# A depthwise convolution rewritten over odd and even tokens, and one norm moved among attention heads

## The chip, the cores and the metric

The kernel runs on one core of one Trainium2 chip. The metric is device time in microseconds (us) of one execution. Five engines run their own instruction streams and meet at semaphores: TensorE (PE, with its weight loads as PEld), VectorE (DVE), ScalarE (ACT), GpSimd (POOL) and SyncE (SP), whose queue here issues nearly all transfers.

## What is computed

One encoder layer on two sequences, a prompt of 512 tokens and a sample of 256, all in float32. After an RMSNorm, one input projection feeds two groups in parallel: latent attention with 8 heads, and a convolution group of 512 channels. Both are normalised, joined and projected back; a SwiGLU feed-forward block and a last norm follow. The part that is changed is the convolution group:

```python
u = conv_a * jax.nn.sigmoid(conv_g)
u = lax.conv_general_dilated(u, dw_w[:, None, :], window_strides=(1,),
                             padding=[(CONV_PAD, CONV_PAD)],
                             dimension_numbers=("NWC", "WIO", "NWC"),
                             feature_group_count=CONV_CH) + dw_b
u = jax.nn.silu(layer_norm(u, conv_ln_g, conv_ln_b))
merged = jnp.concatenate([rms_norm(attn, attn_out_g), rms_norm(u, conv_out_g)], axis=-1)
return merged @ w_out
```

`dw_w` has 31 taps per channel, and each channel is convolved with its own taps, along the tokens, with 15 zeros at both ends of each sequence.

## The kernel before

Products run on TensorE with each operand split into a high and a low part (`split`, lines 104 to 111: ScalarE rounds the high part, VectorE subtracts to get the low one), three matmuls for each product. Tokens are cut into blocks b of 128 (0 to 3 the prompt, 4 and 5 the sample), channels into four tiles i of 128. The program is written in this order:

- A: the convolution's input projection, channel tile by channel tile. `glu(i)` gates a tile: VectorE writes the gated values to `u[s][i]` (s is 0 for the prompt, 1 for the sample), with zeros around them.
- B: the attention's input projections (`tm_mm`), by block. C: queries, keys and values (`q_up`, `k_up`, `v_up`), and the rotary step `rope` (lines 375 to 378) on VectorE after each `q_up`. When C is done, its pools are closed and the memory is given to tiles of the attention, `qh` and `ql` among them, so that the first `qh` waits for the last `rope`.
- D: the attention in 12 units (`units`): units 0 to 3 are the sample's heads in pairs, units 4 to 11 the prompt's heads. A unit is scores (`pss`, line 293), a row maximum on VectorE (`ngmx`, line 711), the exponential on ScalarE (line 714), transposes (`ptp`, line 731) and the product with the values (`po`). The scores have three PSUM banks. The loop writes `st_q(i + 1)`, `st_s(i)`, `st_t(i - 1)` and, for every second head, `st_v(i - 1)` at step i.
- Between these steps of D stand pieces of the convolution's norm: `conv_ln(b)` (four transposes `pcl` of the convolution's result, statistics `bst` and `mv` on VectorE, a reciprocal root on GpSimd, the normalised `z` on ScalarE), `conv_act1` and `conv_act2` (transposes `pca` back, swish, the sum of squares `prc`), `conv_split`. The prompt's start at step `LN0` = 4. The sample's stand at the end: after the last head come the output products `oc(b, o)` of the prompt's convolution half, with `attn_norm` for the prompt, and the sample's `conv_ln(4)`, `conv_ln(5)`, `conv_act1(1, k)`, `conv_act2(1, k)` and `conv_split(1)` lie among `oc(1, 1)` to `oc(3, 1)`.
- Then `out_conv` and `out_attn` for the remaining blocks into eight `bank` tiles, the second norm, and the feed-forward block, which fills the rest of the run from about 355 us.

The convolution is not matmul work. Each output tile `acc[s][i]` starts as tap 0 times u plus the bias on ScalarE (line 248), and 30 VectorE instructions add one tap each:

```python
for j in range(1, KW):
    yield n / 512, lambda j=j: DVE.scalar_tensor_tensor(a, us[:, j : j + n], w(j), a, ALU.mult, ALU.add)
```

These taps fill VectorE between other work. A generator (`conv_taps`) yields a cost and an instruction; every matmul written through `mm` adds its length times a rate (`RATE`, one for each stage) to an account, and `tap_some` writes taps until the account is used up, in turn from the first `TAPW` generators. `tap_all(s)` writes all that are left. The framework then orders each engine's instructions, by readiness and by the order of writing; only transposes written under `pin` keep their place.

## Time and profile before

| | |
|---|---|
| median of three runs | 846.03 us (843.57 to 849.58) |
| the profiled execution | 845.79 us, span 844.0 us |
| TensorE busy | 810.1 us, 96% of the span |
| VectorE busy | 714.8 us, 85% |
| ScalarE busy | 434.4 us, 51% |
| mean granted TensorE clock | 0.990 |

The span runs from the first to the last instruction; the execution's own time is 1.8 us longer. In a timeline row stand the start, the length, the engine, the line, the operation, output<-input, sizes and the number of instructions merged; in brackets is the idle time before it and what ended it. Rows of stretches give for each engine busy time and instructions, then the granted clock (1.00 is full speed), the share of the DMA engines and GB/s. "Landing" is the time from a transfer's issue to its arrival.

### The profile page before, as it was taken

The page shows a single profiled execution, that of the slowest core. Times are in us where ns is not written, and L with a number is a line of the kernel's source. Part 1 is how long each engine was busy: PE and PEld are TensorE (multiplying, and loading weights), DVE is VectorE, ACT ScalarE, POOL GpSimd, SP SyncE. Part 2 cuts the span into 40 slices and gives each one's busy share as a digit, 9 for nine tenths or more (in the row PEclk, how much of TensorE's full clock was granted, in tenths as well). Part 3 has the DMA queues.
Part 4 walks back from the last instruction along what each step waited for, and adds up shares of the span by engine and source line. Part 5 has one row for each costly group of instructions (what it writes and reads, how often), then busy time and mean ns, then how long its engine had stood idle before and what let it go on. Part 6 is the DMA issues. An engine that isn't in the chain of part 4 may idle for free.

```text
span 844.0 us, 12490 instructions
## 1 busy us (share of the span) xinstructions
PE 810.1 (96%) x4381; PEld 722.9 (86%) x4381; DVE 714.8 (85%) x1310; ACT 434.4 (51%) x886; POOL 87.9 (10%) x113
## 2 busy tenths in 40 slices
PE   6999999879999899999999999999999999999996
PEld 5888998866766678799999999999999988888775
DVE  4699989989898855898999988898988669989993
ACT  6623337958895254784333343433334346455753
POOL 1000341001010201100000000000000000004743
PEclk9999999989999989999999999999999999999999
DMA  8812102300001231368554333444344699963344
GB/s 304 293 54 76 45 1 76 151 1 1 1 1 51 75 101 75 114 203 287 191 196 151 122 127 130 147 144 147 126 151 139 218 306 321 312 205 123 103 138 149
DMA packets 49662, 117.18 MB, mean 139 GB/s; under 512 B 5056, under 2 KB 18368, under 8 KB 49600
## 3 DMA queue, kind: packets, MB, share of 16 engines
q1 hardware_dynamic: 49424, 116.00, 40.9%
q8 instruction: 34, 0.56, 0.3%
q10 hardware_dynamic: 144, 0.39, 0.1%
q14 instruction: 28, 0.23, 0.1%
q0 software_dynamic: 32, 0.00, 0.0%
HBM read 93.96 MB, written 22.41 MB: 138 GB/s over the span
## 4 chain that ended last, share of the span: by engine, by line
PE 54%; DVE 4%; issue 3%; DMA 1%; POOL 1%; ACT 1%; POOLq 0%; ACTq 0%; DVEq 0%
PE bank L293 53%; DVE wr L108 1%; DMA sr<-wdn 1%; DVE sr L1308 1%; DVE ra L108 1%; DVE xall L1214 0%; DVE sa L108 0%; DVE xall L1227 0%; PE bank L982 0%; POOL nmv L969 0%; POOL fmv L1241 0%; POOL fmr L1242 0%; DVE vt L1218 0%; POOL nmr L971 0%; ACT vt L1226 0%
## 5 line engine op out<-in xcount | busy, mean ns | idle before, releaser
L293 PE MATMUL bank<-ra,wr 128*128 128x384 f32 x1056 | 186.6, 335 | 0.0
L293 PEld LDWEIGHTS bank<-ra,wr 128*128 128x128 f32 x1056 | 183.4, 188 | 0.0
L293 PE MATMUL bank<-sa,wr 128*128 128x384 f32 x780 | 139.2, 335 | 0.0
L293 PE MATMUL bank<-wr,wr 128*128 128x512 f32 x594 | 135.1, 389 | 1.3 <-DVE wr L108 1.3
L293 PEld LDWEIGHTS bank<-sa,wr 128*128 128x128 f32 x780 | 135.5, 188 | 0.0
L250 DVE SCALAR_TENSOR_TENSOR acc<-u,c,acc 128x512 f32<-128x512 f32 (+1 forms) x240 | 132.9, 610 | 0.1
L293 PEld LDWEIGHTS bank<-wr,wr 128*128 128x128 f32 x594 | 111.4, 188 | 24.8 <-DVE wr L108 1.7
L107 ACT CAST wr<-vt 128x512 fp32r<-128x512 f32 x88 | 54.6, 620 | 97.7 <-PE bank L293 92.6
L107 ACT CAST wr<-sr 128x512 fp32r<-128x512 f32 x106 | 64.7, 616 | 61.3 <-PE bank L293 60.0
L108 DVE TENSOR_TENSOR wr<-sr,wr 128x512 fp32r<-128x512 f32 x106 | 71.9, 683 | 14.7 <-ACT wr L107 14.7
L1236 POOL TENSOR_SCALAR fme<-fms 128x1 f32<-128x1 f32 x6 | 33.9, 5644 | 418.3 <-ACT vt L1226 418.0
L293 PE MATMUL pc<-ra,sa 128*128 128x256 f32 (+1 forms) x288 | 54.4, 350 | 8.2 <-ACT ra L110 8.2
L108 DVE TENSOR_TENSOR wr<-vt,wr 128x512 fp32r<-128x512 f32 x88 | 60.1, 685 | 0.0
L293 PEld LDWEIGHTS pc<-ra,sa 128*128 128x128 f32 x288 | 45.8, 195 | 15.8 <-ACT ra L110 8.6
L107 ACT CAST wr<-ra 128x384 fp32r<-128x384 f32 x51 | 26.0, 512 | 33.1 <-PE bank L293 21.2
L293 PE MATMUL pss<-ra,qh 96*128 96x512 f32 (+1 forms) x96 | 30.4, 397 | 6.2 <-ACT qh L107 5.3
L108 DVE TENSOR_TENSOR wr<-ra,wr 128x384 fp32r<-128x384 f32 x51 | 28.1, 551 | 8.5 <-ACT wr L107 8.3
L293 PE MATMUL bank<-wr,ra 128*128 128x512 f32 x144 | 34.2, 394 | 0.0
L293 PE MATMUL pq<-sa,ra 128*128 128x384 f32 x108 | 33.8, 342 | 0.0
L711 DVE TENSOR_REDUCE ngmx<-pss 128x1 f32<-128x512 f32 (+1 forms) x40 | 27.0, 685 | 6.2 <-PE pss L293 6.0
L293 PEld LDWEIGHTS bank<-wr,ra 128*128 128x128 f32 x144 | 26.7, 188 | 5.6
L293 PE MATMUL bank<-sa,ra 128*128 128x512 f32 x114 | 30.3, 419 | 0.1
(224 smaller groups left out, 1340.5 us busy)
## 6 DMA issues: line engine op xcount, KB each, us to landing
sr<-wgu SPq DMA_DIRECT2D x52, 512.0 KB, 3.9
sr<-wdn SPq DMA_DIRECT2D x34, 512.0 KB, 4.6
sumd<-xall SPq DMA_DIRECT2D x44, 192.0 KB, 1.9
ra<-sumd SPq DMA_DIRECT2D x44, 192.0 KB, 5.0
actd<-xall SPq DMA_DIRECT2D x11, 384.0 KB, 2.3
xall<-actd SPq DMA_DIRECT2D x11, 384.0 KB, 2.9
st<-wconv SPq DMA_DIRECT2D x7, 512.0 KB, 6.1
xr<-xtok SPq DMA_DIRECT2D x6, 512.0 KB, 6.7
```

Of the source, the lines that this page charges most:

```text
L107: ACT.copy(dst_hi, src)
L108: DVE.tensor_sub(dst_lo, src, dst_hi.bitcast(F32))
L250: yield n / 512, lambda j=j: DVE.scalar_tensor_tensor(a, us[:, j : j + n], w(j), a, ALU.mult, ALU.add)
L293: pinned(PE.matmul(out, lhsT, rhs, start=start, stop=stop))
L711: DVE.tensor_reduce(mx, ps.rearrange("p (j n) -> p j n", j=m), AX.X, ALU.max, negate=True)
L1236: POOL.tensor_scalar(fme[b], fms[:, 2 * b + 1 : 2 * b + 2], 1.0, EPS, ALU.mult, ALU.add)
L1308: DVE.tensor_add(w, tw[f], w)
```

## The change

Let e and o be a channel's even and odd taps (16 and 15), and x0, x1 the gated values at every second position of the padded sequence. The 31-tap convolution is then put together from three of half the length: P = x0 with the even taps, Q = x1 with the odd ones, and S = x0 + x1 with the sums of neighbouring taps. The even outputs are P + Q, the odd ones S - P - Q, each plus the bias. Both sequences lie side by side in one row of 416 positions with 16 zeros between them, so that one instruction over 400 or 401 columns serves prompt and sample.

- `glu(i)` writes each gated piece in two instructions, reading every second column, instead of in one. Line 255 and 256 (`cab`) add neighbouring taps once; they are written at `build_rb` and read only the constants `c`.
- Per channel tile, instead of 30 taps of 512 and 30 of 256 columns: one sum x0 + x1 (416), 15 + 14 + 15 taps of 400, one subtraction (400), and four instructions that write outputs to every second column (two of 256, two of 128). ScalarE starts P, Q and S (three of 400) instead of two accumulators (512 and 256).
- `TAPW` is 2 instead of 4. The rate in C is 0.3 instead of 0.6. A tap's cost is 0.81 units (a 512-column tap was 1).
- Because one generator now makes both sequences, all taps must be done where the prompt's norm begins. `LN0` is 6 instead of 4, with `tap_all(0)` there. The sample's `conv_ln` stands at step `LN0` + 3, its `conv_act1` and `conv_act2` at `LN0` + 4, `conv_split(1)` behind the last head, and the output products at the end stand alone.
- The normalised tiles `z` share the two buffers of P, Q and S, two to a buffer, instead of four buffers of their own.

```diff
-RATE = {"A": 0.6, "B": 1.4, "C": 0.6, "D": 1.0, "S": 1.0, "F": 1.2}
+RATE = {"A": 0.6, "B": 1.4, "C": 0.3, "D": 1.0, "S": 1.0, "F": 1.2}
-TAPW = 4
-LN0 = 4
+TAPW = 2
+TAPC = 0.81
+LN0 = 6
...
     def build_rb():
+        tap_sums()
...
+    def tap_sums():
+        w = c[:, C_DW : C_DW + 4 * KW].rearrange("p (i j) -> p i j", i=4)
+        DVE.tensor_add(cab[:, :, :15], w[:, :, 0 : KW - 1 : 2], w[:, :, 1:KW:2])
+        DVE.tensor_copy(cab[:, :, 15:], w[:, :, KW - 1 :])
...
-        ACT.activation(a, us[:, :n], AF.Identity, bias=c[:, C_DB + i : C_DB + i + 1], scale=w(0))
-        for j in range(1, KW):
-            yield n / 512, lambda j=j: DVE.scalar_tensor_tensor(a, us[:, j : j + n], w(j), a, ALU.mult, ALU.add)
+        yield TAPC, lambda: DVE.tensor_add(xs, u0, v1)
+        ACT.activation(P, u0[:, :NP_], AF.Copy, scale=w(0))
+        ACT.activation(Q, v1[:, 1:NP_], AF.Copy, scale=w(1))
+        ACT.activation(S, xs[:, 1:NP_], AF.Copy, scale=ab(0))
...
+        for j in range(1, 16):
+            yield TAPC, lambda j=j: tap(P, u0, j, w(2 * j))
+            if j < 15:
+                yield TAPC, lambda j=j: tap(Q, v1, 1 + j, w(2 * j + 1))
+            yield TAPC, lambda j=j: tap(S, xs, 1 + j, ab(j))
+        yield TAPC, lambda: DVE.tensor_sub(S, S, P[:, 1:])
...
         if i == LN0:
             tap_all(0)
-            pace["s"] = 1.0
-            pin[0] = True
             conv_ln(0)
             conv_ln(1)
-            pin[0] = False
...
         elif i == LN0 + 2:
             for k in range(4):
                 conv_act1(0, k)
                 conv_act2(0, k)
-            for b in range(NB):
-                load_x(b)
-        elif i == LN0 + 4:
             attn_norm(4)
             attn_norm(5)
+        elif i == LN0 + 3:
+            conv_ln(4)
+            conv_ln(5)
             conv_split(0)
-        elif i == LN0 + 7:
+        elif i == LN0 + 4:
+            for k in range(4):
+                conv_act1(1, k)
+                conv_act2(1, k)
             wc0 = conv_w(0)
...
-    oc(0, 1)
-    tap_all(1)
-    oc(1, 1)
-    conv_ln(4)
-    conv_ln(5)
-    oc(2, 1)
-    for k in range(4):
-        conv_act1(1, k)
-    oc(3, 1)
-    for k in range(4):
-        conv_act2(1, k)
-    conv_split(1)
+    for b in range(4):
+        oc(b, 1)
```

Three places show what this does to the order (an x and a number at a row's end count alike instructions in a row). The first is the start of VectorE's stream, where it makes the low parts of the first weights (`sa`) and inputs (`ra`). Before:

```order
L108 TENSOR_TENSOR sa_2_70<-st_151,sa_2_70 128x256
L111 SCALAR_TENSOR_TENSOR ra_69<-st_155,g_81,ra_69 128x512
L111 SCALAR_TENSOR_TENSOR ra_69<-st_155,g_81,ra_69 128x256
L108 TENSOR_TENSOR sa_2_70<-st_161,sa_2_70 128x256
L111 SCALAR_TENSOR_TENSOR ra_69<-st_165,g_81,ra_69 128x512
```

and now:

```order
L109 TENSOR_TENSOR sa_2_70<-st_135,sa_2_70 128x256
L255 TENSOR_TENSOR cab<-c 128x4x15
L256 COPY cab<-c 128x4
L112 SCALAR_TENSOR_TENSOR ra_69<-st_139,g_81,ra_69 128x512
L112 SCALAR_TENSOR_TENSOR ra_69<-st_139,g_81,ra_69 128x256
L109 TENSOR_TENSOR sa_2_70<-st_145,sa_2_70 128x256
```

The two instructions on the taps, which need the constants `c`, now stand ahead of the low part of the first input.

The second place is VectorE between the last maximum of unit 6 and the first of unit 7 (`pss_2215` before and `pss_2163` now are unit 6's last scores). Before, ten taps on the sample (256 columns) stood there ahead of the first swish of the prompt and four behind it; the prompt's statistics were done:

```order
L711 TENSOR_REDUCE ngmx<-pss_2207 128x1
...
L108 TENSOR_TENSOR ql_2190<-ptq_2184,qh_2189 96x512
...
L711 TENSOR_REDUCE ngmx<-pss_2215 128x1
L250 SCALAR_TENSOR_TENSOR acc_116<-u_124,c,acc_116 128x256
...
L605 SCALAR_TENSOR_TENSOR acc_112<-th_2276,yt_2275 128x512
L250 SCALAR_TENSOR_TENSOR acc_118<-u_126,c,acc_118 128x256
```

Now 28 instructions of the convolution stand there (18 taps of 400 or 401 columns, two subtractions and the eight instructions that write `uv_114` and `uv_115`, the channel tiles 2 and 3), and the statistics of the first two blocks behind them, ahead of unit 7's first maximum:

```order
L769 TENSOR_REDUCE ngmx<-pss_2163 128x1
L278 SCALAR_TENSOR_TENSOR pqs_1318<-uv_114,c,pqs_1318 128x401
...
L292 SCALAR_TENSOR_TENSOR uv_114<-pqs_1318,c 128x256
...
L295 SCALAR_TENSOR_TENSOR uv_114<-pqs_1318,c 128x128
...
L295 SCALAR_TENSOR_TENSOR uv_115<-pqs_1611,c 128x128
L109 TENSOR_TENSOR ql_2304<-ptq_2298,qh_2303 96x512
L631 BN_STATS bst_2270<-pcl_2265 128x6
L631 BN_STATS bst_2287<-pcl_2282 128x6
L632 BN_AGGR mv_2271<-bst_2270 128x2
L769 TENSOR_REDUCE ngmx<-pss_2307 128x1
```

On TensorE the same place reads now as follows (`pcl` are the transposes of the convolution's result, `pss_2325` the last scores of unit 7):

```order
L341 MATMUL pss_2319<-ra_69,ql_2140 128x512
L789 MATMUL ptp_2331<-ident,sa_221_1802 128x128 x4
L789 MATMUL ptp_2343<-ident,sa_221_1802 128x128 x4
L628 MATMUL pcl_2265<-ident,uv_114 128x128
L628 MATMUL pcl_2282<-ident,uv_114 128x128
L341 MATMUL po_2451<-sa_221_1802,vt_1443 64x512
L744 MATMUL ptq_2394<-ident,sa_177_1449 96x128 x4
L628 MATMUL pcl_2265<-ident,uv_115 128x128
L628 MATMUL pcl_2282<-ident,uv_115 128x128
L789 MATMUL ptp_2337<-ident,sa_221_1802 128x128 x4
L628 MATMUL pcl_2355<-ident,uv_112 128x128
L341 MATMUL pss_2325<-ra_69,qh_2139 128x512 x2
```

Between unit 6's last scores and the first `pcl` on `uv_114`, TensorE has eight `po` products, five groups of four `ptp` transposes, one of `ptq`, and three sets of scores of unit 7. The transposes of `uv_114` and `uv_115` now stand in the middle of unit 7's work, and the rest of that work behind them.

The third place is TensorE's last output products. Before:

```order
L293 MATMUL pe_2992<-sa_397_2837,ra_69 128x512 x12
L570 MATMUL pcl_3006<-ident,acc_116 128x128
...
L293 MATMUL pe_3040<-sa_397_2837,ra_69 128x512 x12
L590 MATMUL pca_3054<-ident,z_3021 128x128
...
L293 MATMUL pe_3085<-sa_397_2837,ra_69 128x512 x12
L293 MATMUL prc_3099<-ones,th_3058 128x2 x4
L293 MATMUL prc_3099<-ones,th_3073 128x2 x4
L293 MATMUL bank_3125<-sa_387_2738,ra_69 128x512 x12
```

and now:

```order
L341 MATMUL pe_3025<-sa_424_2898,ra_69 128x512 x12
L341 MATMUL pe_3039<-sa_424_2898,ra_69 128x512 x12
L341 MATMUL pe_3053<-sa_424_2898,ra_69 128x512 x12
L341 MATMUL pe_3067<-sa_424_2898,ra_69 128x512 x12
L341 MATMUL bank_3086<-sa_406_2774,ra_69 128x512 x12
```

The sample's `pcl`, `pca` and `prc` are gone from there; they now stand among the scores of units 10 and 11. The number of matmuls is the same, and so is the order of the transfers.

## The prediction

> **What bounds the kernel now.** I read the busy times first, then busy time by stretches (columns: PE, PEld, DVE, ACT, POOL busy and instructions, granted clock, share of the DMA engines, GB/s), then what TensorE waited for.

> ```profile
> PE 810.1 (96%) x4381; PEld 722.9 (86%) x4381; DVE 714.8 (85%) x1310; ACT 434.4 (51%) x886; POOL 87.9 (10%) x113
> ```

> ```profile
> 60.00:70.00 10.00, 10.00 (x58) 8.68 (x58) 9.14 (x16) 3.90 (x6) 0.00 (x0) 1.00 0.44 141
> ...
> 170.00:180.00 10.00, 5.50 (x26) 5.08 (x27) 8.25 (x19) 3.05 (x10) 0.00 (x0) 0.66 0.00 0
> ...
> 230.00:240.00 10.00, 10.00 (x59) 6.31 (x57) 8.96 (x19) 9.21 (x23) 2.76 (x4) 1.00 0.00 0
> ...
> 290.00:300.00 10.00, 8.42 (x46) 6.80 (x46) 4.67 (x11) 5.84 (x14) 1.96 (x6) 1.00 0.00 0
> 300.00:310.00 10.00, 9.38 (x31) 7.65 (x32) 6.88 (x14) 6.94 (x14) 1.59 (x2) 0.66 0.33 107
> ```

> ```profile
> PE pc L293 <- ACT ra L110: 8.2, 2, 6.0
> PE pss L293 <- ACT qh L107: 5.3, 1, 5.3
> ...
> PE pca L590 <- ACT z L579: 1.3, 2, 0.8
> PE pcb L656 <- DVE z L644: 1.2, 2, 0.7
> ...
> PE prc L293 <- ACT th L606: 0.9, 2, 0.6
> PE pcl L570 <- DVE acc L250: 0.8, 1, 0.8
> PE pss L293 <- ACT sa L714: 0.7, 1, 0.7
> ...
> PE pcl L570 <- ACT z L579: 0.6, 1, 0.6
> ```

> TensorE bounds it: 34 of 844 us are idle, and its matmuls stay the same in number. VectorE's 85% is cover for the taps, so fewer VectorE microseconds are worth nothing by themselves. Only three things can be won or lost: idle time of TensorE, time at half clock, and the start. Half clock stands in two stretches, a mean of 0.66 over 10 us each, which is 6.8 us at 0.5. The first follows the 5.3 us hole at the entry to the attention, the second the small holes of the sample's norm at 288 to 301 us (`pca`, `prc`, and `pcl` behind the last tap).

> **VectorE's work.** In place of 240 taps stand 176 taps of 400 columns and some helpers.

> ```profile
> 99.60 6.04 DVE L250 SCALAR_TENSOR_TENSOR acc<-u,c,acc 128x512 f32<-128x512 f32 x9
> ```

> ```profile
> 260.51 5.23 DVE L250 SCALAR_TENSOR_TENSOR acc<-u,c,acc 128x256 f32<-128x256 f32 x13
> ```

> ```profile
> L108 DVE TENSOR_TENSOR cq<-ptq,cq 128x384 fp32r<-128x384 f32 x6 | 3.3, 551 | 3.8 <-ACT cq L107 3.8
> ```

> Back to back a 512-column tap takes 0.67 us and a 256-column one 0.40. That is 1.05 ns a column on a fixed 0.13, so 400 columns take 0.55 us and 128 some 0.27. Before: 120 x 0.67 + 120 x 0.40 = 128 us. After, for each channel tile: 44 taps x 0.55 = 24.2, the sum and the subtraction 1.1 (from the 384-column row), four outputs 2 x 0.40 + 2 x 0.27 = 1.3; 26.6, times four 106 us. The gating in two halves adds about 0.13 us eight times. VectorE loses some 20 us of 128. The writes to every second column have no row; I take the dense price, bounded above by twice that, 1.3 us more for a tile. [...]

> **The start: +1.3 us.** `cab` waits for the constants and stands ahead of the low part of the first input.

> ```profile
> 2.10 0.44 SPq L218 DMA_DIRECT2D c<-cst  x1
> ...
> 7.17 0.33 SPq L216 DMA_DIRECT2D st<-xT  x1
> ```

> ```profile
> c<-cst SPq DMA_DIRECT2D x1, 174.5 KB, 5.0
> ```

> ```profile
> 6.00 1.15 DVE L111 SCALAR_TENSOR_TENSOR ra<-st,g,ra 128x512 fp32r<-128x512 f32 x2 [0.74 <-ACT ra L110]
> ```

> ```profile
> 19.08 13.18 PE L293 MATMUL pc<-ra,sa 128*128 128x512 f32 x72 [2.23 <-ACT ra L110]
> ```

> The constants land at 2.10 + 5.0 = 7.1 us; with two tiny instructions the low part starts at about 7.35 instead of 6.00. Queued behind it are every later low part and, through the staging buffers that VectorE frees, SyncE's next input (issued at 7.17, just as that part ends). TensorE's wait at 19.08 is for such an input, so it moves by as much: 1.3 us. Lower end 0 (the transfer queue still had work), upper 1.6.

> **A to C: nothing.** From 19 to 130 us TensorE has no wait, and by the order VectorE has as much work before the first rotary step as before, since the account writes as many microseconds of shorter taps. The hole at the entry to the attention stays:

> ```profile
> 172.75 0.28 DVE L378 TENSOR_TENSOR sa<-rc,rs 128x128 f32<-128x128 f32 x1
> ```

> ```profile
> 173.14 1.07 ACT L107 CAST qh<-ptq 96x512 fp32r<-96x512 f32 x2 [5.81 <-DVE sa L378]
> ```

> ```profile
> 150.75 15.67 PE L293 MATMUL pqu<-sa,cq 128*128 128x384 f32 x89 [1.14 <-DVE ra L498]
> ...
> 173.77 1.65 PE L293 MATMUL pss<-ra,qh 96*128 96x256 f32 x6 [5.31 <-ACT qh L107]
> ```

> `qh` waits for the last rotary step because it takes its memory. VectorE ran almost without a gap up to it, the taps among its work. Between the last key rotation and the last query rotation stand now 37 taps and outputs, about 20 us, where 31 taps took 20 us; the halved rate in C is made up by taps left over from B. So 0; at best the step is done as soon as its input is (166.4 + 1.0 for ScalarE's copies + 1.3 for its four instructions), 4 us earlier, and the 2.1 us of half clock with it (below), together -6; at worst +1.

> **Unit 6 to 7: +6.1 us of holes, +2.1 of half clock.** Here `tap_all` leaves 28 instructions in one piece: 18 x 0.55 + 2 x 0.55 + 4 x 0.40 + 4 x 0.27 = 13.7 us. What TensorE has meanwhile is priced by these rows:

> ```profile
> 213.02 2.79 PE L293 MATMUL po<-PT,vt 128*64 128x512 f32 x10
> 215.74 1.09 PE L590 MATMUL pca<-ident,z 128*128 128x128 f32 x8
> 216.66 0.60 PE L686 MATMUL ptq<-ident,sa 128*96 128x128 f32 x4
> ...
> 218.25 0.63 PE L293 MATMUL pss<-ra,qh 96*128 96x512 f32 x2
> ...
> 218.95 0.62 PE L293 MATMUL pss<-ra,qh 96*128 96x512 f32 x2
> ```

> ```profile
> 198.87 1.30 DVE L573 BATCH_NORM_STATS2 bst<-pcl 128x6 f32<-128x512 f32 x2 [0.19 <-PE pcl L570]
> ```

> ```profile
> 202.40 0.66 PE L570 MATMUL pcl<-ident,acc 128*128 128x128 f32 x4 [0.58 <-ACT z L579]
> ```

> A float32 `po` is two passes of 0.27, a transpose 0.115 (8 in 0.92), a set of three scores 0.70. Counted from unit 6's last score: eight `po` 4.3, five groups of transposes and one `ptq` 2.75, three sets 2.1, together 9.2 us; then two `pcl`, a `po` and a `ptq` (1.2). In the heads before, such work runs some 8% slower: from unit 3's last maximum to unit 11's lie 68 us,

> ```profile
> 188.96 0.69 DVE L711 TENSOR_REDUCE ngmx<-pss 128x2 f32<-128x512 f32 x1 [0.21 <-PE pss L293]
> ```

> ```profile
> 257.27 0.68 DVE L711 TENSOR_REDUCE ngmx<-pss 128x1 f32<-128x512 f32 x1
> ```

> and by the order they hold 32 sets of scores (22), the `po` (15), 193 transposes (22) and 16 `prc` (a pair of passes like a transpose, 3), 63 us. So TensorE is through at 11.2. Tile 3 is ready after the maximum (0.6) and 13.7, at 14.3: 3.1 us of holes. Then 1.1 us of transposes; the third `pcl` waits for a bank, which needs statistics, GpSimd and `z`, and that took 3.5 us from the first statistics (198.87 to 202.40). They start at 14.9 behind one `ql`, so it runs at 18.4: 3.0 us more, where before this chain was covered by scores and cost 0.6. Scores of unit 7 are queued behind these transposes. Lower end 3 (ScalarE holds TensorE back in any case), upper 9. In this stretch TensorE works half the time; at 288 to 301 us holes of at most 0.8 us were enough for half clock. I add what the first half-clock stretch cost, 173.8 to 178.0 at half: 2.1; bounds 0 and 3.2. [...]

> **The end: -6.2 us.** The holes of the sample's norm go: `pca` 1.3, `prc` 0.9, `pcl` 0.8, 3.0 us; and the half clock after 301, in which TensorE was busy: 6.8 x 0.94 / 2 = 3.2. The `pcb` waits stay. Among the heads the sample's norm has scores as cover; without it, 2.2 come back. The single `pcl` wait in the heads goes into the hole above: -0.6.

> **Sum.** +1.3 + 6.1 + 2.1 - 6.2 - 0.6 = +2.7. The span of the profiled execution, 844.0, becomes 846.7; with the 1.8 us around it 848.5. That execution lies 0.2 under the median of 846.03.

> **Rivals.** About 1% (8.5 us) can be told from no change.

> *VectorE gets ahead.* If a 400-column tap costs 0.44 or less, the last rotary step is done 37 x 0.11 = 4 us sooner and the entry hole closes as far as it can (-6, with its half clock); the piece at unit 6 shrinks by 18 x 0.11 = 2 us, its holes fall to their lower end (-3), and no half clock follows there (-2.1): 837 us. For it: 22% fewer columns than in a prompt tap. Against it: 256 columns already take 0.40, and the two rows give 0.55.

> *ScalarE becomes the bound in units 7 to 11.* The prompt's `z` and swish come two heads later, and the sample's come into the heads, most of the 5.8 us that the row at 290 shows for ScalarE. The row at 230 has it busy 9.2 of 10 us; over the 50 us of these units that is 46, and 52 with the sample's, against some 54 of TensorE. Where ScalarE cannot absorb it, the scores wait behind the swish in its queue: 5.8 more, and the holes at unit 6 grow by 2 since `z` and the exponentials compete: 856 us. It decides once ScalarE is over 95% busy there. Against it: the holes at unit 6 give it idle time.

> *The shorter taps save nothing.* At 0.67 a tap the entry hole grows by 4 and the piece by 2: 855 us. The 256-column row speaks against it.

> **How the numbers follow.** The forecast, within 1%, has 0.58; VectorE ahead 0.2 (the two holes that it closes need no cheap tap if the order leaves VectorE more slack than I count); ScalarE 0.18, the dear taps 0.04. So faster 0.2, same 0.58, slower 0.22. The range of 836 to 857 reaches to the price of both main rivals; the forecast alone, from its bounds at unit 6, has 843 to 852.

> **What would show it.** Right: `ra` waits for `c` at the start and TensorE's wait before 20 us is longer by about 1.3; the `qh` hole is 4 to 7 us; a run of 28 convolution instructions of about 14 us on VectorE, with `pcl` waiting for `uv` and for `z` 3 us each; no wait between the last head and the `bank` products but `pcb`; VectorE busy some 20 us less. Wrong: an entry hole under 2 us, no `pcl` wait above 1 us, or a ScalarE that is waited for in every head.

## The result, and the profile after

The changed kernel takes 856.24 us (four executions, 855.80 to 857.20) against 845.27 of the kernel before beside it: a ratio of 1.0108, 95% interval 1.0061 to 1.0155 (the two medians alone give 1.0130, which the interval holds). A second comparison gave 1.0097 (1.0062 to 1.0131). The forecast was 848.5 with a range of 836 to 857: the range holds the time, but the likeliest course, "within 1%", was about 8 us too fast. Unless another kernel is named, the rows below are of the changed kernel's profiled execution (855.95 us, span 853.9).

TensorE stays the bound, and VectorE has lost 18.6 us of work:

```profile
PE 817.7 (96%) x4381; PEld 729.9 (85%) x4381; DVE 696.2 (82%) x1280; ACT 437.1 (51%) x890; POOL 78.6 (9%) x109
```

To see where the 9.9 us of span arose, I cut both spans at the same four events: the first score, the end of unit 6's last maximum, the first `bank` product, and the first of the 1056 products `bank<-ra,wr`. First the kernel before, then the changed one (columns as in the prediction's stretches):

```profile
0.00:173.77 173.77, 157.40 (x920) 143.44 (x920) 149.00 (x275) 91.90 (x189) 24.82 (x49) 0.99 0.35 121
173.77:210.70 36.93, 35.62 (x224) 27.34 (x224) 32.10 (x66) 29.25 (x82) 4.04 (x12) 0.94 0.00 1
210.70:302.04 91.34, 86.06 (x458) 59.13 (x457) 77.45 (x162) 61.77 (x140) 10.27 (x20) 0.99 0.09 29
302.04:390.10 88.06, 85.90 (x434) 76.32 (x435) 69.69 (x115) 53.78 (x109) 8.30 (x14) 0.97 0.46 156
390.10:844.00 453.90, 445.16 (x2350) 416.68 (x2348) 386.58 (x697) 197.66 (x369) 40.53 (x18) 1.00 0.53 175
```

```profile
0.00:175.00 175.00, 158.81 (x924) 144.56 (x924) 149.56 (x313) 93.43 (x193) 19.37 (x45) 1.00 0.36 120
175.00:209.26 34.26, 33.97 (x194) 26.02 (x194) 29.18 (x50) 26.21 (x78) 0.00 (x0) 0.86 0.00 1
209.26:314.96 105.70, 96.72 (x483) 68.37 (x483) 66.36 (x119) 70.68 (x152) 13.46 (x34) 0.90 0.14 44
314.96:400.10 85.14, 83.05 (x433) 74.25 (x432) 64.08 (x105) 48.87 (x101) 6.61 (x12) 1.00 0.39 139
400.10:853.90 453.80, 445.15 (x2351) 416.70 (x2349) 387.06 (x696) 197.94 (x369) 39.19 (x18) 1.00 0.53 175
```

The differences are +1.2, -2.7, +14.4, -2.9 and -0.1. The heads, rows two and three, hold all of it: +11.7 from the first score to the first `bank` product (the matmuls that left the second row stand in the third, since the prompt's norm comes two heads later). Split by TensorE's state: idle 6.6 before and 9.3 now, +2.7. Lost to half clock, which is one minus the clock, times the busy time: 0.06 x 35.62 + 0.01 x 86.06 = 3.0 before, 0.14 x 33.97 + 0.10 x 96.72 = 14.4 now, +11.4. The rest of the busy time is -2.4, which I have not traced. **Nearly the whole loss is TensorE working at half clock, not TensorE waiting.**

What it waits for, in part:

```profile
PE pss L341 <- ACT qh L108: 5.5, 1, 5.5
PE pss L341 <- ACT sa L772: 2.9, 5, 0.8
...
PE pcl L628 <- ACT z L637: 1.4, 1, 1.4
PE pcl L628 <- DVE uv L295: 1.4, 1, 1.4
...
PE prc L341 <- ACT th L664: 1.0, 2, 0.6
```

The `qh` hole at the entry is as long as before. The waits at unit 6 and the new ones for exponentials (`sa`) are single holes of at most 1.4 us.

The granted clock shows more. In the records of this execution its four half-clock stretches last one, two or three times 3.41 us (below), so I set stretches on that grid. The row before the half clock, its three parts and the row behind, in units 8 and 9:

```profile
246.01:249.43 3.42, 3.42 (x29) 3.02 (x27) 2.55 (x6) 2.71 (x6) 0.00 (x0) 1.00 0.00 0
249.43:252.84 3.41, 2.48 (x16) 1.72 (x14) 2.40 (x5) 2.98 (x8) 1.08 (x2) 1.00 0.00 0
252.84:256.25 3.41, 3.29 (x14) 2.85 (x14) 0.93 (x4) 1.28 (x5) 0.61 (x1) 0.50 0.00 0
256.25:259.67 3.42, 2.92 (x10) 2.25 (x10) 2.08 (x4) 3.05 (x8) 2.37 (x7) 0.50 0.00 0
259.67:263.08 3.41, 3.41 (x15) 2.96 (x14) 1.30 (x3) 2.47 (x6) 1.00 (x3) 0.50 0.02 5
263.08:266.49 3.41, 2.81 (x14) 1.51 (x13) 3.20 (x6) 3.41 (x10) 0.00 (x0) 1.00 0.00 0
```

TensorE is busy 2.48 of 3.41 us in the stretch ahead, yet the clock halves. Its instructions there:

```profile
249.65 0.99 PE L341 MATMUL prc<-ones,th 128*128 128x2 f32 x8
250.50 0.48 PE L341 MATMUL pss<-ra,ql 96*128 96x512 f32 x1
250.82 0.60 PE L628 MATMUL pcl<-ident,uv 128*128 128x128 f32 x4
252.18 0.49 PE L341 MATMUL pss<-ra,qh 96*128 96x512 f32 x1 [0.76 <-ACT sa L772]
```

Eight of them are `prc`, which stream two columns each: about 0.12 us of "busy" apiece, where a `pss` of 0.48 us streams 512. All half-clock stretches up to the `bank` products: from 174.3 us (three parts), 225.5 (two), 252.8 (three), 280.2 (one); before: 171.2 (two) and 300.9 (two).

### The profile page after: what moved, and what is told of

The parts are those of the page before. It is cut to its first block, busy times and chain, and to the rows that moved or that the text cites. A ratio compares the mean times of both kernels' runs of the same rounds, so it can differ in the third digit from the quotient of the medians.

```text
span 853.9 us, 12452 instructions
## 1 busy us (share of the span) xinstructions
PE 817.7 (96%) x4381; PEld 729.9 (85%) x4381; DVE 696.2 (82%) x1280; ACT 437.1 (51%) x890; POOL 78.6 (9%) x109
## 4 chain that ended last, share of the span: by engine, by line
PE 76%; DVE 11%; ACT 4%; issue 4%; DMA 3%; POOL 1%; SPq 0%; POOLq 0%; ACTq 0%; DVEq 0%
PE bank L341 50%; PE pc L341 7%; PE pss L341 3%; PE pq L341 3%; PE pe L341 3%; DVE wr L109 2%; PE pt L341 2%; DVE pqs L278 2%; PE po L341 2%; PE ptp L789 2%; DMA sr<-wdn 1%; ACT ra L507 1%; DMA st<-xT 1%; DVE xall L1265 1%; DVE sr L1359 1%
## 5 line engine op out<-in xcount | busy, mean ns | idle before, releaser
L108 ACT CAST wr<-vt 128x512 fp32r<-128x512 f32 x88 | 54.6, 621 | 98.3 <-PE bank L341 95.3
L108 ACT CAST wr<-sr 128x512 fp32r<-128x512 f32 x106 | 64.7, 616 | 61.5 <-PE bank L341 59.8
L278 DVE SCALAR_TENSOR_TENSOR pqs<-uv,c,pqs 128x401 f32<-128x401 f32 (+1 forms) x116 | 68.2, 627 | 0.0
L108 ACT CAST wr<-ra 128x384 fp32r<-128x384 f32 x51 | 26.1, 513 | 36.0 <-PE bank L341 24.5
L341 PE MATMUL pss<-ra,qh 96*128 96x512 f32 (+1 forms) x96 | 35.0, 445 | 8.4 <-ACT qh L108 5.5
L278 DVE SCALAR_TENSOR_TENSOR pqs<-xs,cab,pqs 128x400 f32<-128x400 f32 x60 | 36.4, 626 | 0.1
```

The lines of the kernel that those rows point to most:

```text
L108: ACT.copy(dst_hi, src)
L278: DVE.scalar_tensor_tensor(d, x[:, o : o + n], sc, d, ALU.mult, ALU.add)
L341: pinned(PE.matmul(out, lhsT, rhs, start=start, stop=stop))
```

## The experiments

Two readings stood against each other. **The clock**: TensorE's clock falls where little streams through it, and the change gathered such work (`prc`, lone transposes between waits) in units 7 to 11. **ScalarE**: the last heads run at ScalarE's pace, and the half clock only follows its waits.

A ratio is to the kernel before on the same chip, with its 95% interval. "Lost" is one minus the mean granted clock, times the span, averaged over all executions of a kernel (it includes some 3 us behind the last product, and not the slow start, the first 9 to 14 us, of which the trace has no clock record). The last column is the start of the first `bank<-ra,wr` product in the one profiled execution; behind it no edit changes anything.

| | ratio (interval) | lost, us | `bank<-ra,wr` from, us |
|---|---|---|---|
| before | 1 | 9.4 | 390.1 |
| changed (second run: after_again) | 1.0097 (1.0062 to 1.0131) | 16.7 | 400.5 |
| wide_norm | 1.0046 (1.0018 to 1.0074) | 10.2 | 395.0 |
| sample_last | 1.0131 (1.0097 to 1.0166) | 15.6 | 400.9 |
| no_piece | 1.0179 (1.0151 to 1.0207) | 20.0 | 406.3 |
| sums_gpsimd | 1.0104 (1.0068 to 1.0140) | 17.1 | 400.0 |
| before_wide | 0.9935 (0.9911 to 0.9959) | 7.6 | 389.5 |
| before_filled | 0.9984 (0.9962 to 1.0006) | 5.7 | 393.9 |
| before_fill8 | 0.9987 (0.9960 to 1.0014) | 5.6 | 387.6 |
| after_filled | 1.0081 (1.0054 to 1.0108) | 6.4 | 397.1 |
| wide_ln7 | 0.9952 (0.9926 to 0.9978) | 6.1 | 388.9 |
| wide_sample_last | 1.0024 (1.0006 to 1.0043) | 10.0 | 392.1 |
| wide_ln7_fill8 | 0.9990 (0.9966 to 1.0014) | 7.1 | 388.9 |

**wide_norm**: the products `prc` with 128 columns.

```diff
-            mm(
-                pr[:, 2 * b : 2 * b + 2], th[:, b * 128 : (b + 1) * 128], ones[:, :2],
+            pinned(PE.matmul(
+                pr[:, 128 * b : 128 * b + 128], th[:, b * 128 : (b + 1) * 128], ones,
...
-            v[:, :nb], pr[:, : 2 * nb].rearrange("p (b two) -> p b two", two=2)[:, :, 0],
+            v[:, :nb], pr[:, : 128 * nb].rearrange("p (b m) -> p b m", m=128)[:, :, 0],
```

> The changed kernel, with one edit: the products `prc` take all 128 columns of `ones` instead of 2 (the same sums, 128 equal columns of them). Theory one, the clock: 8.5 of the 9.9 us lost are work at half clock, and the stretches that begin at 252 and 280 us follow the `prc`, which stream two columns each and so leave TensorE all but idle although it counts as busy. With 128 columns both stretches go: 4.8 + 1.7 = 6.5 us less, some 850 us. Theory two, ScalarE sets the pace of the last heads (`pss` waits 2.9 us for exponentials, `prc` 1.0 for ScalarE's squares): nothing that ScalarE does changes, so 856 us, within 1, and the half clock stays where it was.

Both stretches went; one single part appeared at 261.9 us, behind waits of `pca` (1.5) and `pss` (0.6). Lost clock fell from 16.7 to 10.2 us, the `bank<-ra,wr` products came 5 us sooner, and of the waits for exponentials 1.0 us is left of 2.9. This stretch of wide_norm holds eight `prc` too and the clock stays up (it has no wait either, so by itself it proves little):

```profile
248.27:251.68 3.41, 3.41 (x30) 3.15 (x29) 3.10 (x6) 3.41 (x11) 1.17 (x4) 1.00 0.00 0
```

ScalarE's work is the same. This speaks for the clock.

**before_wide**: the same edit in the kernel before the change.

> The kernel before the change, with one edit: `prc` takes 128 columns of `ones` instead of 2. Theory one, the clock goes by how much TensorE streams in each stretch of 3.41 us: the half clock after 300.5 us goes, 3.3 us of 844 and a ratio of 0.996 to the kernel before. Theory two, the half clock comes from the waits for ScalarE at the sample's norm: they stay, so does the half clock, ratio 1.000 within 0.002.

The half clock behind 300.9 us is gone, with `pca` and `prc` still waiting for ScalarE (1.4 and 0.7 us). The ratio fell further than expected (0.9935, not 0.996), although its profiled execution happened to have four parts of half clock at the entry. Of these 5.5 us the clock, averaged over all executions, explains 1.8 (9.4 less 7.6); where the rest comes from is not shown. This version is faster than the kernel before, and nothing done to the changed kernel went below its ratio.

**sample_last**: the sample's norm back at the end; only the convolution, its place and the prompt's norm stay as changed.

```diff
         elif i == LN0 + 3:
-            conv_ln(4)
-            conv_ln(5)
             conv_split(0)
...
-    for b in range(4):
-        oc(b, 1)
+    oc(0, 1)
+    oc(1, 1)
+    conv_ln(4)
+    conv_ln(5)
...
```

> The changed kernel, with the sample's norm (its `pcl`, `pca`, `prc` and split) back behind the heads, in the places where it stood before the change; the convolution stays in halves. Theory one, the clock: the stretch at 280 us goes (1.7), the one at 252 stays or loses one part of it (0 to 1.7), the waits of `prc` and `pss` at the sample's norm go (1.5), and at the end 3.0 us of holes and 3.2 of half clock return: 856 to 859 us. Theory two, ScalarE: 5.8 us of ScalarE's work leave units 8 to 11, the waits and the half clock there go as a whole (2.9 + 6.5), and the end costs 6.2: 853 us.

ScalarE's reading fails: without the sample's work in the heads, the waits for exponentials are as long, and the half clock at 252.9 us again has three parts. The clock's reading missed too: it had some of these waits go and 3.2 us of half clock return at the end. The holes did return there (`pca` 1.4, `prc` 0.9), and no half clock followed.

```profile
PE pss L341 <- ACT sa L772: 3.0, 4, 1.2
```

The move of the sample's norm by itself was worth little or nothing: 1.0131 against 1.0097 to 1.0108. With wide `prc` the sign is the other way:

> The changed kernel with the wide `prc`, and the sample's norm back behind the heads. If the cost of the change lies in the convolution's piece and its waits, this place is worth what it was with narrow `prc` (0.2% slower than among the heads): 1.0046 to 1.008. Rival: the sample's norm among the heads is itself what costs, through ScalarE; then the ratio falls towards that of the kernel before with the wide `prc`, 0.998 or less.

wide_sample_last has 1.0024 against wide_norm's 1.0046, between what the two readings expected; the intervals overlap, so this place decides nothing that can be told apart.

**no_piece**: the rate of convolution work in B at 2.4 instead of 1.4.

> The changed kernel, with the rate of convolution work in stage B at 2.4 instead of 1.4, which by the order leaves no piece of 28 convolution instructions at unit 6, and 26 instead of 37 of them between the last key rotation and the last query rotation. Theory one, holes and clock at unit 6: the waits of `pcl`, `ptp` and `ptq` there (4.6 us) and the half clock behind them (2.8) go, 7.4 less, 849 us; up to 6 less again if the hole at the entry to the attention shrinks with the 11 instructions. Rival: VectorE is full from 50 to 130 us, so the key rotations come up to 13 us later, TensorE gets new waits in B and C, and nothing is won: 856 to 862 us.

The rival came true. No half clock stands at unit 6 any more, but the work that went ahead of the rotary steps made new holes in C and half clock with them, three parts from 133 us on:

```profile
PE pku L341 <- ACT zk L464: 7.5, 1, 7.5
...
PE pku L341 <- ACT zq L458: 2.6, 1, 2.6
```

**wide_ln7**: wide `prc`, and LN0 = 7, which breaks the piece into 10, 4 and 14.

> The changed kernel with the wide `prc`, and LN0 at 7 instead of 6: the piece of 28 convolution instructions falls into 10, 4 and 14, with maxima between, and the norm of both sequences comes one head later. If the piece at unit 6 costs what its waits (4.6 us) and its half clock (2.8) say, half of it goes: 3 to 5 us less than the wide `prc` alone, ratio 1.000. Rival: the waits only move one head on, and the norm has fewer heads as cover: 1.0046 to 1.008.

Between unit 6 and the `bank` products no half clock is left, and those waits at unit 6 that the piece made (`pcl` for `uv`, `pcl` for `z`) are gone (new ones of `ptp` come to 2.7 us); against wide_norm the `bank<-ra,wr` products begin 6.1 us sooner. That is more than the 3 to 5 us expected, and near what the waits (4.6) and the half clock (2.8) of the piece said, so the rival fails. The part at 261.9, up to 1.7 us, is gone as well, and LN0 moves both norms with the piece: how much belongs to the piece alone is not separated. Its line of products, beside that of wide_norm:

```profile
L341 PE MATMUL bank<-ra,wr x1056: 338/338/338, 388.9 to 677.1; 128*128 128x384 f32 x176
```

```profile
L341 PE MATMUL bank<-ra,wr x1056: 335/335/335, 395.0 to 677.7; 128*128 128x384 f32 x176
```

The two ended at almost the same time, because each of these products took 338 ns in one execution and 335 in the other (see the end).

**sums_gpsimd**: the two `cab` instructions on GpSimd.

> The changed kernel, with the two instructions that form `cab` on GpSimd instead of VectorE, so that no low part of an input waits for the constants. If the start costs what its waits show, the first wait of TensorE comes 0.6 to 1.3 us sooner and the whole is 855 us. Rival: what is won at the start is taken back at the entry to the attention, where TensorE waits for VectorE in any case: 856 us; the half-clock stretches may begin elsewhere, 1.7 us for each part of 3.4 us.

No input's low part waits for the constants any more, and TensorE still waits 2.44 us at 19.23 (2.23 at 19.08 before the change): nothing was won.

```profile
19.23 4.96 PE L341 MATMUL pc<-ra,sa 128*128 128x512 f32 x18 [2.44 <-ACT ra L111]
```

The half clock lies otherwise, with a single part even at 19.5 us.

**before_filled, after_filled, before_fill8, wide_ln7_fill8**: all four with the wide `prc`, and with idle products in the entry hole (15 or 8), in after_filled also ahead of the last transposes of two `pcl`.

```diff
+            if un == 0 and b == 0:
+                for _ in range(15):
+                    PE.matmul(ps[:, :C_N], ident, c, start=True, stop=True)
...
+            if b < 2 and i == 3:
+                for _ in range(10):
+                    PE.matmul(pt[:, 384:], ident, PTs[LN0 - 1][0][:, :128], start=True, stop=True)
```

> The kernel before the change with the wide `prc`, and 15 idle products (`ident` by 349 columns of `c`, into the bank of the first scores, which overwrite it) in the hole at the entry to the attention. Theory one, by streaming: no half clock is left up to 320 us, 2.1 + 3.3 = 5.4 us less, ratio 0.9936; the hole itself stays, full of products without use. Rival: the products outlast the hole or the clock falls in any case: not under the ratio of the kernel with the wide `prc` alone, and up to 1 us above it.

> The changed kernel with the wide `prc`, the 15 idle products at the entry to the attention, and 10 more ahead of the last transpose of each of the first two `pcl` at unit 6, into columns that the transpose overwrites. Theory one, by streaming: the stretches that began at 173 and 224 us (4.5 and 2.8 us lost) go too, ratio 1.0046 - 0.0086 = 0.996; the waits themselves stay. Rival: the half clock follows the waits whatever TensorE streams in them: 1.0046 or, where the products stand in the way, up to 1.007.

The clock did most of what the streaming theory says: in after_filled it stays full through the hole and at unit 6 (single parts are left at 184.5 and 263.0 us). But 15 products were to fill a hole of 5.5 us, 0.37 each, and they took 0.60: they outlasted the hole by 2.5 us, and by the new order a transpose then waited 4 us for a maximum. Both ratios missed: before_filled 0.9984 where 0.9936 was expected, after_filled 1.0081, above even the rival's 1.007.

```profile
168.51 8.97 PE L767 MATMUL pss<-c,ident 128*128 128x349 f32 x30
...
184.03 0.33 PE L796 MATMUL ptp<-ident,sa 128*128 128x128 f32 x1 [3.98 <-DVE ngmx L776]
```

> The kernel before the change with the wide `prc` and 8 idle products at the entry to the attention instead of 15: by the run with 15 one takes 0.60 us, so 4.8 us, which ends inside the hole of 5.3. Theory one, by streaming: no half clock behind the hole, 2 to 4 us less than with the wide `prc` alone, ratio 0.990. Rival: what cost the time with 15 was not their length but the order behind them (the scores of a bank now stand together, and `ptp` waits 3.6 us for a maximum): ratio 0.9935 to 0.998.

> The changed kernel with the three edits that each took time off: the wide `prc`, LN0 at 7, and 8 idle products at the entry to the attention. Before this stage the products `bank<-ra,wr` began at 388.9 us with the first two edits, against 390.1 in the kernel before the change. Theory one, by streaming: the half clock behind the entry falls from three parts of 3.41 us to two or fewer, these products begin at 386 to 387 us, ratio 0.992 to 0.994. Rival: as in the kernel before, a wait of `ptp` for a maximum (2.0 us) takes the place: 388 to 390 us, ratio 0.995 to 0.999.

With 8 they fit. In wide_ln7_fill8 the half clock at the entry is gone altogether, but two parts now stand at 264.5, amid new waits of `pss` (2.1) and `pca` (2.3) for ScalarE; in before_fill8 two parts stand at 181, behind a wait of 2.0 us for a maximum. Neither gained by the ratio over the kernel without the products (0.9987 against 0.9935, 0.9990 against 0.9952), and both missed the 0.990 to 0.994 expected of the streaming theory. So less lost clock did not become less time here: that the products keep the clock up is shown, that they pay is not. For before_fill8 the profiled start of the `bank<-ra,wr` products (387.6, the earliest of all) and the ratio disagree; this stays open.

**after_again**, the changed kernel a second time:

> The changed kernel itself, beside the others on the same chip: a ratio of 1.0108, as in the first comparison. If the clock is decided on a grid of 3.41 us that does not start with the kernel, the half-clock stretches again last 1, 2 or 3 times 3.41 us and stand whole multiples of it apart, but some of them begin elsewhere or are of another length.

It had the same stretches, with 3, 2, 3 and 1 parts, each 0.5 us later; none began elsewhere or changed its length, as I had thought possible.

## Why the prediction was right and wrong

- **VectorE's work: right.** Three 401-column taps stand in 1.71 us, 0.547 each from start to start (0.55 forecast); a strided output of 256 columns took 0.40, the dense price. VectorE lost 18.6 us (20 forecast).

```profile
209.17 1.71 DVE L278 SCALAR_TENSOR_TENSOR pqs<-uv,c,pqs 128x401 f32<-128x401 f32 x3
...
215.66 0.48 DVE L292 SCALAR_TENSOR_TENSOR uv<-pqs,c 128x256 f32<-128x256 f32 x1
216.06 0.62 DVE L278 SCALAR_TENSOR_TENSOR pqs<-uv,c,pqs 128x400 f32<-128x400 f32 x1
```

- **The start, +1.3: wrong, and hidden by luck.** The wait is there and the low part starts at 7.46, as worked out.

```profile
7.25 0.22 DVE L255 TENSOR_TENSOR cab<-c 128x60 f32<-128x60 f32 x1 [1.87 <-DMA c<-cst]
7.39 0.17 DVE L256 COPY cab<-c 128x4 f32<-128x4 f32 x1
7.46 1.14 DVE L112 SCALAR_TENSOR_TENSOR ra<-st,g,ra 128x512 fp32r<-128x512 f32 x2
```

But ahead of 22 us TensorE waits 8.2 us in all, as before, and sums_gpsimd shows that without `cab` nothing is won: the lower bound, 0, was right. The first score does come 1.2 us later, for another reason: TensorE starts at a slow pace in both executions, to 13.9 us here and to 10.7 before (a 512-column product takes 0.63 us up to there and 0.39 behind), some 1.5 us of work. In the same half microsecond TensorE, busy throughout, does 5 products before (first row) and 3 now; the clock column, 1.00 in both, has no record of this start.

```profile
11.50:12.00 0.50, 0.50 (x5) 1.00 1.04 401
```

```profile
11.50:12.00 0.50, 0.50 (x3) 1.00 1.27 240
```

- **A to C, 0: right**, and the entry hole stayed (5.45 us, forecast 5.3). What I left out: its half clock, two parts before, need not stay at two. It took three: 4.7 us lost between 175 and 209 us against 2.1 before.

- **Unit 6 to 7, +6.1 of holes and +2.1 of half clock: right in kind.** The piece ran from 209.17 to 222.60, 13.4 us (13.7 forecast). TensorE's holes were 0.73 + 1.36 at the tiles and 0.43 + 0.68 + 1.39 at `z`, together 4.6, and two parts of half clock followed, in which it was busy 5.6 us, so 2.8 lost. wide_ln7 puts the whole at about 6.1 us.

```profile
218.67 0.65 PE L789 MATMUL ptp<-ident,sa 128*128 128x128 f32 x4 [0.73 <-ACT sa L791]
...
222.48 0.44 PE L628 MATMUL pcl<-ident,uv 128*128 128x128 f32 x2 [1.36 <-DVE uv L295]
223.34 0.66 PE L789 MATMUL ptp<-ident,sa 128*128 128x128 f32 x4 [0.43 <-DVE ql L109]
224.68 0.66 PE L789 MATMUL ptp<-ident,sa 128*128 128x128 f32 x4 [0.68 <-ACT PT L791]
226.72 1.11 PE L628 MATMUL pcl<-ident,uv 128*128 128x128 f32 x4 [1.39 <-ACT z L637]
```

- **The end, -6.2: right at its place.** No wait stands between the last output products and `bank`, and the last stage is 2.9 us shorter (3.2 of half clock forecast).

- **The failed step is the clock term.** I put the half clock behind 301 us down to "the small holes of the sample's norm" and took it as won when these go: "Among the heads the sample's norm has scores as cover". The idle time came out as a sum (+2.7 from the first score to `bank`, forecast 6.1 - 3.0 - 0.6 = 2.5), but by errors that cancel: the holes at unit 6 were 1.5 us shorter, while the `prc` kept its waits (1.0 us, forecast 0) and those for exponentials grew from 0.7 to 2.9. The clock does not come out: one stretch of 2.1 us was forecast there, and 11.4 came (2.5 more at the entry, 2.8 at unit 6, 4.8 from 252.8 and 1.7 from 280.2 us, less 0.4 before). wide_norm and before_wide show the cause that I had missed: the 2-column `prc`. The half clock moved with them, and the prompt's `prc` got it too: four groups 3 us apart did no harm at 217 to 227 us before, while at 250 the same meet a wait of 0.8 (1.2 in sample_last, where the sample's transposes are not there). The 4.8 and 1.7 went with wide `prc`, the 2.8 with the piece; the 2.5 at the entry are a third part behind much the same hole (5.45 us here, 5.31 before). So the row at 301, with half clock behind holes of at most 0.8 us, was the right one to go by, but I drew from it one more stretch instead of asking which of its instructions the change moves.

- **The rivals.** The time fell on "ScalarE becomes the bound" (856 us), but not by its mechanism: ScalarE was busy at most 9.17 of 10 us, under the 95% from which I let it decide, and sample_last leaves the loss in place. A right number for a wrong reason.

```profile
260.00:270.00 10.00, 9.40 (x45) 6.21 (x43) 5.56 (x10) 9.17 (x20) 1.00 (x3) 0.85 0.01 2
```

## What to carry to other kernels

Count what TensorE streams, not what the profile calls busy (here half clock followed a stretch of 3.41 us that was 73% busy): price every move of tiny products and lone transposes by what else flows in the same few microseconds. A product with two columns, padded to 128, took 0.02 us more here (275 against 251 ns), and with it the lost clock fell from 16.7 to 10.2 us (wide_norm). With that repair in both kernels the changed one, its piece broken up too, stands at 0.9952 and the one before at 0.9935: the 18.6 us of VectorE work that the change saves bought no time that can be told. When a change moves work into a covered place, look for its clock there as well as its waits, and where a long piece of one engine's work must be done by a due time, break it up at that time rather than push it ahead of other due work.

## What the runs showed of the hardware

**Half clock came in parts of 3.41 us.** In 14 profiles the 36 half-clock stretches between the start and the end last one to four times 3.41 us, and all those of one execution lie whole multiples of 3.41 apart. Where the grid lies differs: the first full clock comes at 13.9 us in the changed kernel, at 10.7 in the one before, and nearly the same entry hole (5.3 to 5.5 us) cost two, three or four parts (before, changed, before_wide).

**The pace of products differs between executions.** A 384-column `bank` product took 335, 336 or 338 ns, from execution to execution, at a full granted clock and in the same kernel (the changed one: 335, then 336). Over the 1836 products of these two groups, 3 ns are 5.5 us, as much as most effects here; that is why the table has the start of the first of them beside the ratio. Where the pace comes from stays open.
